# Query latent moved out of the first loop, the section behind it ordered by the scheduler, three gates early

## Chip, cores and metric

The kernel runs on one core of one Trainium2 chip. The metric is the device time of one execution in microseconds (us). All shapes are written partitions x elements; everything is stored as 32-bit floats.

## The reference

One layer of a diffusion block over 512 tokens of width 1024, with 256 context tokens. Cut to what matters here:

```
hx = rms_norm(x) * (1 + scale) + shift          # shift, scale = silu(c) @ w_mod, per channel
hc = rms_norm(ctx) * (1 + scale_c) + shift_c
conv_x, qa, kva, kr, gates = split(hx @ w_in)   # 2048, 384, 256, 64, 2048 columns
kva_c, kr_c = hc @ w_in[:, kv and kr columns]
q   = rms_norm(qa)  @ w_uq                      # 8 heads, 128 plain + 64 rotary
k,v = rms_norm(kva) @ w_ukv                     # 8 heads, keys and values, also for kva_c
att = softmax(q k) v @ w_o
u   = a * sigmoid(g);  y = silu(layer_norm(conv31(u))) @ w_pw
x  += m2 * ((sigmoid(g_conv) * y + sigmoid(g_mla) * att) @ w_out)
x  += m5 * swiglu(rms_norm(x) * (1 + m4) + m3);   out = rms_norm(x)
```

## The kernel before

Channels lie on partitions in tiles of 128, tokens along the free axis. Every product is made of three matmuls: weight and activation are each split into a high part (float32r, made by ScalarE, line 116 for weights) and a low part (the rest, made by VectorE, line 120), and `mm3` (L131) adds high*high, high*low and low*high. A weight of 128x1024 is loaded by SP into one of three raw buffers (`wr`), then split into two `wh` and two `wl` tiles of 512; with W_BUFS = 6 there are three such sets in all. The tag `x` of PSUM has 4 buffers of 512, the tag `s` 2 of 1024. A tile's buffer comes free when its last reader is done.

Order of work. Inside `manual_schedule` (L516 to L749) each engine runs the instructions in the order of the text. Outside it the order is made at build time by the framework's scheduler: the place in the text is the importance, and of the instructions whose operands and buffer are there by the scheduler's own estimate the most important is queued next on its engine. Each engine then runs its queue strictly in that order, SP's and POOL's DMA issues included.

The stages around the change:

- *Start* (L517 to L543). SP loads x, the row of c and, for k = 0 to 3, `load_mod(k)`: two halves of w_mod0, one tile of w_mod1 and one of w_q. ScalarE and VectorE square and add x; PE runs 34 warming matmuls (`warm`), sums the squares (`colsum`, L181), makes the shift of tile 0 and 1 with matmuls of 2 columns (`shift_dots`, L261, 16 instructions each) and spreads 1/rms over the partitions (`spread`, L171). Nine more warming matmuls stand ahead of the loop.
- *First loop* (L545 to L587), k = 0 to 7. VectorE and ScalarE make tile k of hx (L563, L564, L570); VectorE makes the scale of the next tile as a row dot product (L257); PE adds 18 matmuls (L572, L583, L585) to six accumulators `accx`: two for the query latent (one more at accx[5]), two for the kv latent, one for the rotary key. w_q therefore has 768 columns. One group of shift dots stands in each step.
- *Section behind it* (L588 to L749), written out by hand: squares, sums and 1/rms of the kv and query latents (`squares`, `added`, `diag`, `bcast` at L625, `latent_t` at L634, `latent_lo` at L641), the rotary key (L404, L419), the two convolution inputs u0 and u1 (`conv_steps`, L301; 48 matmuls each at L298) pumped in pieces between them, eight row dots for the context scale (`ctx_dots`, L593), the context tiles `hcs` (L712, L715, L718), two gates (`gate_steps`, L488) whose result goes to DRAM through POOL (L493), the context latent `pkv` and key `pkr`, and the first head's query, keys and values (`prep_qr`, `prep_qn`, `prep_kx`, `prep_kc`, `prep_v`).
- *Heads* (L752 to L771): scores, taps of the convolution, attention. Behind them (L773 to L803) five gates of the attention, the mean over the convolution (L790), the other six gates of the convolution and the norm; `spill` is read back at L787.

Of the kernel before, what the change touches and what calls it, by code (L numbers as in the profile page):

```python
# [10 lines left out]
F32 = mybir.dt.float32  # L11
F32R = mybir.dt.float32r
# [6 lines left out]
P = 128  # L19
# [14 lines left out]
WK_AT = (2, 5)  # L34
# [6 lines left out]
EARLY = 2  # L41
# [12 lines left out]
def block_kernel(ctx: ExitStack, tc: tile.TileContext, I, out):  # L54
# [461 lines left out]
    with tc.manual_schedule(engines={ET.PE, ET.DVE, ET.Activation, ET.Pool, ET.SP}):  # L516
# [18 lines left out]
        r = rstd_cols(st, D, 4)  # L535
        scale_dot(0)
        shift_dots(0)
        w = w_slots(768)
        w_hi(w, wq[0])
        ss = shift_scale(0)  # L540
        bc = spread(r, 4, tiny)
        shift_dots(1)
        warm(WARM[1])  # L543
        rx = slot()
        for k in range(KD):  # L545
# [7 lines left out]
            if k == 4:  # L553
# [6 lines left out]
                load_c += [load_w(I["w_in"][3 + KD + 1])]  # L560
# [7 lines left out]
            if nxt:  # L568
                scale_dot(k + 1)
            dve.scalar_tensor_tensor(out=hl, in0=t, scalar=ss[:, 0:1], in1=hh.bitcast(F32), op0=ALU.add, op1=ALU.subtract)  # L570
            for j in range(6):
                pe.matmul(accx[j], lhsT=wc(w[0], j * P), rhs=hh, start=k == 0, stop=False)  # L572
            if nxt:
                w2 = w_slots(768)
# [7 lines left out]
            for j in range(6):  # L582
                pe.matmul(accx[j], lhsT=wc(w[1], j * P), rhs=hh, start=False, stop=False)  # L583
            for j in range(6):
# [3 lines left out]
        mds = [load_md(k) for k in range(4)]  # L588
        load_c.append(load_w(I["w_in"][3 + 1]))
        act.activation(ccrow, ccrow, AF.Silu)  # L590

        def ctx_dots():
            for k in range(KD):  # L593
                row_dot(mds[k], ccrow, mod_s[:, 24 + k:25 + k])
                if k + 4 < KD:
                    mds.append(load_md(k + 4))
                yield

        dots = ctx_dots()


        def squares(srcs, n):
            o = []
            for p_ in srcs:
                sq = slot(n=n)
                act.activation(sq, p_, AF.Square)
                o.append(sq)
            return o

        def added(o):  # L610
            for sq in o[1:]:
                dve.tensor_tensor(out=o[0], in0=o[0], in1=sq, op=ALU.add)
            return o[0]

        def diag(r, n):
            dg = slot(n=n)
            dve.tensor_tensor(
                out=dg.rearrange("p (b j) -> p b j", b=n // P),
                in0=ident.unsqueeze(1).to_broadcast([P, n // P, P]),
                in1=r.unsqueeze(2).to_broadcast([P, n // P, P]), op=ALU.mult)  # L620
            return dg

        def bcast(dg, n):
            bc = tiny(n)
            pe.matmul(bc, lhsT=ones, rhs=dg, start=True, stop=True)  # L625
            o = slot(n=n)
            act.copy(o, bc)  # L627
            return o

        def latent_t(srcs, g, bc, dst, n):  # L630
            ts = []
            for i, s_ in enumerate(srcs):
                t = slot(n=n)
                dve.scalar_tensor_tensor(out=t, in0=s_, scalar=v(g, i), in1=bc, op0=ALU.mult, op1=ALU.mult)  # L634
                act.copy(dst[i][0], t)
                ts.append(t)
            return ts

        def latent_lo(ts, dst):
            for i, t in enumerate(ts):  # L640
                dve.tensor_tensor(out=dst[i][1], in0=t, in1=dst[i][0].bitcast(F32), op=ALU.subtract)  # L641

        for n_, lst in ((2, kva), (3, qa)):
            for _ in range(n_):
                lst.append((slot(F32R), slot(F32R)))
        krh, krl = slot(F32R), slot(F32R)
        krc = slot(F32R)
        for _ in range(2):
            h_ = slot(F32R)
            kvac.append((h_[:, 0:C], h_[:, C:2 * C]))  # L650

        misc = tiny()
        st_kv, st_q, st_c, st_c2 = misc[:, 0:4], misc[:, 4:8], misc[:, 8:10], misc[:, 10:12]
        raw8 = []
        steps = conv_steps(0, cw[0], cw[1])
        u0 = next(steps)
        kq = squares(accx[2:4], S)
        qq = squares([accx[5], accx[0], accx[1]], S)
        q2 = slot()
        act.copy(q2, accx[5])  # L660
        kq = added(kq)
        qq = added(qq)
        pump(steps, 12)
        colsum(st_kv, kq, 4, True, True)
        r_kv = rstd_cols(st_kv, 256, 4)
        tk = rope_ts(accx[4])
        pump(steps, 6)
        colsum(st_q, qq, 4, True, True)
# [516 lines left out]
```

## Time and profile before

| what | value |
|---|---|
| median of 3 runs | 1047.76 us (1047.34 to 1049.23) |
| profiled execution: its own time | 1044.45 us |
| profiled execution: span of the core | 1042.7 us |
| mean granted TensorE clock | 0.985 of full |

The span is what the trace covers; the execution's own time is 1.75 us more. A line of a timeline gives start, duration, engine, line of the code, operation, out<-in, shape and count; in square brackets stands how long the engine had stood idle and who ended that. A line of a table by windows gives for each engine the busy time and (x) the number of instructions, then the granted TensorE clock as a share of full speed, the busy share of the DMA engines and their GB/s.

### The profile page before, as it was taken

The page shows a single profiled execution, that of the slowest core. Times are in us where ns is not written, and L with a number is a line of the kernel's source. Part 1 is how long each engine was busy: PE and PEld are TensorE (multiplying, and loading weights), DVE is VectorE, ACT ScalarE, POOL GpSimd, SP SyncE. Part 2 cuts the span into 40 slices and gives each one's busy share as a digit, 9 for nine tenths or more (in the row PEclk, how much of TensorE's full clock was granted, in tenths as well). Part 3 has the DMA queues.
Part 4 walks back from the last instruction along what each step waited for, and adds up shares of the span by engine and source line. Part 5 has one row for each costly group of instructions (what it writes and reads, how often), then busy time and mean ns, then how long its engine had stood idle before and what let it go on. Part 6 is the DMA issues. An engine that isn't in the chain of part 4 may idle for free.

```text
span 1042.7 us, 14009 instructions
## 1 busy us (share of the span) xinstructions
PE 1008.4 (97%) x5178; PEld 854.9 (82%) x5178; DVE 554.7 (53%) x994; ACT 438.3 (42%) x818; POOL 150.6 (14%) x294
## 2 busy tenths in 40 slices
PE   8997999999999999997999999999999999999996
PEld 7885788888888887886878888988888888888886
DVE  5655774555555455426887775744643333433332
ACT  4244365555555556533382233443333333322322
POOL 0000301443443525530000000300000000000000
PEclk8998999999999999999999999999999999999998
DMA  9931742644644616753637654133632222333312
GB/s 343 369 110 40 241 128 76 151 128 121 161 114 128 163 41 160 187 135 112 202 119 254 221 165 150 62 102 104 219 101 92 90 102 95 87 91 108 91 56 81
DMA packets 52852, 143.40 MB, mean 138 GB/s; under 512 B 8880, under 2 KB 11056, under 8 KB 52784
## 3 DMA queue, kind: packets, MB, share of 16 engines
q1 hardware_dynamic: 42384, 116.54, 34.5%
q0 software_dynamic: 10400, 25.97, 10.4%
q8 instruction: 41, 0.67, 0.3%
q14 instruction: 27, 0.22, 0.1%
HBM read 114.42 MB, written 2.62 MB: 112 GB/s over the span
## 4 chain that ended last, share of the span: by engine, by line
PE 88%; DVE 3%; DMA 3%; issue 2%; ACT 2%; POOL 1%; SPq 0%; POOLq 0%; DVEq 0%; ACTq 0%
PE px L132 13%; PE px L133 12%; PE px L134 12%; PE ps L133 9%; PE ps L132 9%; PE ps L134 9%; PE px L298 8%; PE ps L455 3%; PE px L475 2%; PE ps L456 1%; PE px L264 1%; DMA ur<-u 1%; DMA a<-e 1%; PE px L419 1%; PE px L183 1%
## 5 line engine op out<-in xcount | busy, mean ns | idle before, releaser
L120 DVE TENSOR_TENSOR wl<-wr,wh 128x512 fp32r<-128x512 f32 (+2 forms) x284 | 189.9, 676 | 255.4 <-ACT wh L116 248.4
L116 ACT CAST wh<-wr 128x512 fp32r<-128x512 f32 (+2 forms) x290 | 174.4, 610 | 312.2 <-PE ps L133 144.5
L132 PE MATMUL px<-a,wh 128*128 128x512 f32 (+1 forms) x591 | 218.6, 371 | 0.6 <-ACT a L99 0.6
L133 PE MATMUL px<-a,wh 128*128 128x512 f32 (+1 forms) x591 | 217.0, 368 | 2.1 <-DVE a L718 2.1
L134 PE MATMUL px<-a,wl 128*128 128x512 f32 (+1 forms) x591 | 216.8, 367 | 0.0
L133 PE MATMUL ps<-a,wh 128*128 128x512 f32 (+1 forms) x376 | 141.6, 377 | 0.8 <-DVE a L925 0.8
L132 PE MATMUL ps<-a,wh 128*128 128x512 f32 (+1 forms) x376 | 141.5, 376 | 0.0
L134 PE MATMUL ps<-a,wl 128*128 128x512 f32 (+1 forms) x376 | 141.2, 375 | 0.0
L133 PEld LDWEIGHTS px<-a,wh 128*128 128x128 f32 x591 | 111.5, 189 | 22.3 <-DVE a L718 2.7
L132 PEld LDWEIGHTS px<-a,wh 128*128 128x128 f32 x591 | 111.6, 189 | 20.5 <-ACT a L99 1.4
L134 PEld LDWEIGHTS px<-a,wl 128*128 128x128 f32 x591 | 111.5, 189 | 18.2
L168 POOL TENSOR_TENSOR s<-s,mhalf 128x2 f32<-128x2 f32 (+1 forms) x10 | 9.0, 904 | 646.7 <-DVE s L166 646.7
L298 PE MATMUL px<-a,wh 128*128 128x512 f32 x288 | 91.9, 401 | 0.4 <-ACT a L627 0.4
L318 POOL DMA_DIRECT2D ur<-u x128 | 67.9, 537 | 121.2 <-issue 59.5
L133 PEld LDWEIGHTS ps<-a,wh 128*128 128x128 f32 x376 | 70.7, 188 | 14.3 <-DVE a L925 1.5
L134 PEld LDWEIGHTS ps<-a,wl 128*128 128x128 f32 x376 | 70.8, 188 | 12.8
L132 PEld LDWEIGHTS ps<-a,wh 128*128 128x128 f32 x376 | 70.8, 188 | 12.7
L332 POOL DMA_DIRECT2D a<-e x128 | 63.0, 498 | 90.8 <-ACT e L330 69.8
L298 PEld LDWEIGHTS px<-a,wh 128*128 128x128 f32 x288 | 54.6, 193 | 12.6 <-ACT a L627 1.1
L455 PE MATMUL ps<-a,a 128*128 128x512 f32 x160 | 58.2, 400 | 0.0
L298 PE MATMUL px<-a,wl 128*128 128x512 f32 x144 | 57.7, 401 | 0.0
L206 DVE SCALAR_TENSOR_TENSOR a<-p,sc,a 128x512 f32<-128x512 f32 x56 | 40.7, 748 | 19.3 <-DMA p<-in_w_mod_dram 19.1
(199 smaller groups left out, 1436.6 us busy)
## 6 DMA issues: line engine op xcount, KB each, us to landing
wr<-in_w_dram SPq DMA_DIRECT2D x60, 512.0 KB, 3.5
wr<-in_w_in_dram SPq DMA_DIRECT2D x35, 512.0 KB, 4.7
ur<-u POOLq DMA_DIRECT2D x128, 130.0 KB, 3.6
p<-in_w_mod_dram SPq DMA_DIRECT2D x64, 256.0 KB, 4.2
md<-in_w_mod_dram SPq DMA_DIRECT2D x16, 512.0 KB, 6.3
a<-e POOLq DMA_DIRECT2D x128, 64.0 KB, 2.0
a<-in_w_mod_dram SPq DMA_DIRECT2D x16, 256.0 KB, 7.2
wr<-in_w_dwx_dram SPq DMA_DIRECT2D x8, 512.0 KB, 4.0
```

The source lines that it names most:

```text
L116: act.copy(h, raw[:, i * WB:i * WB + h.shape[-1]])
L120: (eng or dve).tensor_tensor(out=l, in0=raw[:, i * WB:i * WB + h.shape[-1]], in1=h.bitcast(F32), op=ALU.subtract)
L132: pe.matmul(ps, lhsT=wh, rhs=ah, start=first, stop=False)
L133: pe.matmul(ps, lhsT=wh, rhs=al, start=False, stop=False)
L134: pe.matmul(ps, lhsT=wl, rhs=ah, start=False, stop=last)
L183: pe.matmul(ps[:, b:b + 1], lhsT=sq[:, b * P:(b + 1) * P], rhs=ones[:, 0:1], start=first and b == 0, stop=last and b == nb - 1)
L206: dve.scalar_tensor_tensor(out=acc[e], in0=md, scalar=sc[:, 2 * kc:2 * kc + 1], in1=acc[e], op0=ALU.mult, op1=ALU.add)
L298: pe.matmul(ps, lhsT=l, rhs=r, start=k == 0 and i == 0, stop=k == n - 1 and i == 2)
L318: pool.dma_start(out=ur[32 * s_:32 * s_ + 32].bitcast(F32), in_=u[32 * g:32 * g + 32, :, 8 * s_:8 * s_ + UW].bitcast(F32))
L332: pool.dma_start(out=parts[j][32 * g:32 * g + 32, :], in_=e[32 * j:32 * j + 32, j:j + S])
L455: pe.matmul(s[:, 0:512], lhsT=l[:, q0:q0 + P], rhs=rx_, start=i == 0, stop=i == 4)
L475: pe.transpose(pt[:, qb * P:(qb + 1) * P], ps_[qb][:, kb * P:(kb + 1) * P], ident)
```

## The change

In the first loop the accumulators of the query latent are gone: `accx` has three entries (two kv, one rotary key), the weight is `w_kv` with 384 columns, and a step has 9 matmuls. The shift dots of tile k + 1 stand in step k ahead of its matmuls (before: those of tile k + 2, in the middle of step k); tile 1's stood ahead of the loop before. Nine warming matmuls move ahead of `spread`, three more stand ahead of the loop. The query latent is made behind the loop by three ordinary products (`gemm`) with tiles `w_qa` of 128x1024, whose raw loads are issued in step 4; each result is squared and copied from PSUM. Loads of the convolution's weights in the loop are gone.

`manual_schedule` now ends with the loop. The section behind it stands in the order: kv latent and rotary key, query latent, context (row dots, `hcs`, pkv, pkr), both convolution inputs whole, `prep(0)`, and `EARLY` = 3 gates whole; the third gate (24 matmuls) leaves the stage behind the heads. No piece is pumped between others by hand.

```diff
-EARLY = 2
+EARLY = 3
...
-        t = wide()
-        sp.dma_start(out=t, in_=I["w_q"][k])
+        t = wide()[:, 0:384]
+        sp.dma_start(out=t, in_=I["w_kv"][k])
...
-    ab = (ps_s(), ps_s())
-    accx = [ab[j // 2][:, (j % 2) * 512:(j % 2) * 512 + 512] for j in range(4)] + [ps_x(), ps_x()]
+    ab = ps_s()
+    accx = [ab[:, 0:512], ab[:, 512:1024], ps_x()]
...
+        shift_dots(0)
+        warm(WARM[1])
+        w = w_slots(384)
+        w_hi(w, wq[0])
+        bc = spread(r, 4, tiny)
         scale_dot(0)
-        shift_dots(0)
-        w = w_slots(768)
-        w_hi(w, wq[0])
         ss = shift_scale(0)
-        bc = spread(r, 4, tiny)
-        shift_dots(1)
-        warm(WARM[1])
+        warm(WARM[2])
...
-            if k == 3:
+            if k == 4:
+                raw_q = [load_w(I["w_qa"][j]) for j in range(3)]
+                sp.dma_start(out=cst[:, 128:1152], in_=I["cst"][:, 128:1152])
                 ccrow = row_tile(1)
-                sp.dma_start(out=cst[:, 128:1152], in_=I["cst"][:, 128:1152])
-                load_c = [load_w(I["w_in"][3 + o]) for o in (KD, 0)]
...
             if nxt:
+                shift_dots(k + 1)
                 scale_dot(k + 1)
...
-            for j in range(6):
+            for j in range(3):
                 pe.matmul(accx[j], lhsT=wc(w[0], j * P), rhs=hh, start=k == 0, stop=False)
...
-            if k + 2 < KD:
-                shift_dots(k + 2)
-            if k >= KD - 2:
-                cw.append(split_w(load_c[k - KD + 2]))
...
+    colsum(st_kv, added(squares(accx[0:2], S)), 4, True, True)
+    wqa = [split_w(raw_q[0])]
+    dg_kv = diag(rstd_cols(st_kv, 256, 4), S)
+    tk = rope_split(rope_ts(accx[2]))
...
+    bc_kv = bcast(dg_kv, S)
+    latent_lo(latent_t(accx[0:2], "g_kv", bc_kv, kva, S), kva)
+    qsrc, qq = [], []
+    for j in range(3):
+        ps = ps_x()
+        gemm(ps, wqa[j], hx)
+        if j < 2:
+            wqa.append(split_w(raw_q[j + 1]))
+        qq += squares([ps], S)
+        t = slot()
+        act.copy(t, ps)
+        qsrc.append(t)
+    colsum(st_q, added(qq), 4, True, True)
+    mds = [load_md(k) for k in range(4)]
+    cq = squares(ctxs, C)
+    for i, sq in enumerate(cq):
+        colsum(st_c, sq, 2, i == 0, i == KD - 1)
+    bc_q = bcast(diag(rstd_cols(st_q, 384, 4), S), S)
+    latent_lo(latent_t(qsrc, "g_q", bc_q, qa, S), qa)
+    rc = bcast(diag(rstd_cols(st_c, D, 2), C), C)
+    for k in range(KD):
+        row_dot(mds[k], ccrow, mod_s[:, 24 + k:25 + k])
+        if k + 4 < KD:
+            mds.append(load_md(k + 4))
...
+    for k in range(KD):
...
+        act.activation(hcs[k][0], t, AF.Identity, bias=ssc[:, k:k + 1])
...
+    pkv = ps_x()
+    for j in range(2):
+        gemm(pkv[:, j * C:(j + 1) * C], wtile(I["w_in"][1 + j]), hcs)
...
+    pkr = ps_x(C)
+    gemm(pkr, wtile(I["w_in"][0]), hcs)
+    split(pkr, krc[:, 0:C], krc[:, C:2 * C])
+    us = []
+    for i in range(2):
+        it = conv_steps(i)
+        us.append(next(it))
+        pump(it, 99)
+    prep(0)
+    for i in range(EARLY):
+        gate_ws[i] = wtile(I["w_in"][19 + i])
+        pump(gate_steps(i), 99)
...
-        for i in range(2, 7):
+        for i in range(EARLY, 7):
             sg_conv.append(gate(19 + i, o_t[6]))
```

## Rows read from the trace of the kernel before

**Rows 1.** The page: its head and the chain that ended last, by engine.
```profile
span 1042.7 us, 14009 instructions
...
PE 88%; DVE 3%; DMA 3%; issue 2%; ACT 2%; POOL 1%; SPq 0%; POOLq 0%; DVEq 0%; ACTq 0%
```

**Rows 2.** Busy time by window: first loop, section behind it, densest 20 us of VectorE.
```profile
26.00:69.60 43.60, 43.60 (x241) 37.65 (x241) 25.26 (x47) 14.83 (x37) 0.00 (x0) 1.00 0.77 282
69.60:148.24 78.64, 68.68 (x357) 57.41 (x355) 56.34 (x104) 37.82 (x77) 14.49 (x28) 0.93 0.43 128
...
100.00:120.00 20.00, 19.51 (x78) 15.98 (x79) 17.18 (x34) 5.19 (x10) 5.61 (x12) 0.89 0.83 251
```

**Rows 3.** The chain in order of time, one step of the loop: start, us, what.
```profile
51.35 1.68 PE px L264 x16
...
57.27 1.68 PE px L264 x16
```

**Rows 4.** Timeline of PE behind the section's first part: matmul spacing, idle time, small sums.
```profile
83.42 3.63 PE L183 MATMUL px<-ones,a 128*128 128x1 f32 x32
...
93.39 0.39 PE L298 MATMUL px<-a,wl 128*128 128x512 f32 x1
...
94.07 0.39 PE L298 MATMUL px<-a,wl 128*128 128x512 f32 x1
100.49 1.22 PE L625 MATMUL px<-a,ones 128*128 128x256 f32 x2 [6.03 <-DVE a L617]
...
123.76 0.28 PE L132 MATMUL px<-a,wh 128*128 128x256 f32 x1
125.94 0.38 PE L133 MATMUL px<-a,wh 128*128 128x256 f32 x1 [1.90 <-DVE a L718]
```

**Rows 5.** Busy time by window: granted clock (third column from the end) at three places.
```profile
16.00:17.00 1.00, 0.00 (x0) 0.00 (x0) 0.96 (x4) 0.87 (x3) 0.00 (x0) 0.50 1.03 414
...
25.00:26.00 1.00, 1.00 (x7) 1.00 (x7) 1.00 (x3) 0.00 (x0) 0.00 (x0) 0.51 1.05 396
...
88.00:89.00 1.00, 1.00 (x4) 0.81 (x3) 0.00 (x0) 0.00 (x0) 0.00 (x0) 0.50 0.83 225
...
103.00:104.00 1.00, 1.00 (x3) 0.78 (x3) 1.00 (x3) 0.00 (x0) 0.00 (x0) 0.50 0.89 311
```

**Rows 6.** Timeline of PE ahead of the loop.
```profile
13.39 1.93 PE L264 MATMUL px<-sc,a 128*128 128x2 f32 x16
17.05 2.07 PE L178 MATMUL px<-t,ones 128*128 128x512 f32 x2 [1.74 <-DVE t L173]
18.92 3.41 PE L264 MATMUL px<-sc,a 128*128 128x2 f32 x16
22.19 4.06 PE L274 MATMUL px<-ones 128*128 128x128 f32 x18
26.00 1.17 PE L572 MATMUL ps<-a,wh 128*128 128x512 f32 x4
```

**Rows 7.** Groups of VectorE in 69.60:148.24: line, operation, count | busy us, mean ns.
```profile
L120 DVE TENSOR_TENSOR wl<-wr,wh 128x512 fp32r<-128x512 f32 x22 | 14.3, 687 | 4.7 <-ACT wh L116 4.6
L257 DVE SCALAR_TENSOR_TENSOR md<-md,row 128x1024 f32<-128x1024 f32 x8 | 9.6, 1222 | 0.1
L712 DVE SCALAR_TENSOR_TENSOR t<-a,ssc,a 128x256 f32<-128x256 f32 x8 | 3.8, 478 | 0.0
```

**Rows 8.** Timeline of POOL: the root of two sums.
```profile
95.95 0.70 POOL L168 TENSOR_TENSOR s<-s,mhalf 128x2 f32<-128x2 f32 x1 [18.36 <-DVE s L166]
...
132.86 1.10 POOL L168 TENSOR_TENSOR s<-s,mhalf 128x2 f32<-128x2 f32 x1 [3.62 <-DVE s L166]
```

**Rows 9.** Timelines behind the heads: PE at the mean, VectorE's last sum, PE's next sum.
```profile
487.12 2.05 PE L790 MATMUL px<-a,ones 128*128 128x512 f32 x2 [5.54 <-DVE a L782]
...
498.40 0.69 DVE L797 TENSOR_TENSOR a<-a,t 128x512 f32<-128x512 f32 x1
...
516.79 0.95 PE L183 MATMUL px<-ones,a 128*128 128x1 f32 x8
```

More of the change, by code (lines that the diff above doesn't have):

```diff
@@ L610, in added @@
[L610 to L656, printed above, removed]
@@ L686, in block_kernel @@
-        pump(steps, 99)
-        raw8 += [load_w(I["w_in"][19 + i]) for i in range(EARLY)]
-        tq = latent_t([accx[0], accx[1], q2], "g_q", bc_q, qa, S)
-        r_c = rstd_cols(st_c, D, 2)
-        cw += [split_w(load_c[3])]
-        latent_lo(tq, qa)
-        dg_c = diag(r_c, C)
-        pump(dots, 4)
-        gate_ws[0] = split_w(raw8[0])
-        load_w8 = [load_w(I["w_in"][1]), load_w(I["w_in"][2]), load_w(I["w_uq"][0, :, 0:D]), load_w(I["w_in"][0]),
-                   load_w(I["w_uv"][0], 512)]
@@ L725, in block_kernel @@
-        pump(gates, 99)
-        pkv = ps_x()
-        for j in range(2):
-            gemm(pkv[:, j * C:(j + 1) * C], wk[j], hcs)
-        wu = split_w(load_w8[2])
-        kq = squares([pkv[:, 0:C], pkv[:, C:2 * C]], C)
-        pump(steps, 5)
-        colsum(st_c2, added(kq), 2, True, True)
-        r_c2 = rstd_cols(st_c2, 256, 2)
-        wkr = split_w(load_w8[3])
-        dg_c = diag(r_c2, C)
-        pump(steps, 99)
-        terms = prep_qr(*wu)
-        prep_qn(*wu, 0)
-        bc_c = bcast(dg_c, C)
@@ L740, in block_kernel, with squares @@
-        pkr = ps_x(C)
-        gemm(pkr, wkr, hcs)
-        latent_lo(latent_t([pkv[:, 0:C], pkv[:, C:2 * C]], "g_kv", bc_c, kvac, C), kvac)
-        wv = split_w(load_w8[4], 512)
-        split(pkr, krc[:, 0:C], krc[:, C:2 * C])
-        stack_q(0, terms)
-        kx = prep_kx(*wu, 768)
-        stack_q(1, terms)
-        prep_kc(*wu, 768, 0, kx)
-        prep_v(*wv, 0)
-    us = [u0, u1]
+    def squares(srcs, n):
+        o = []
+        for p_ in srcs:
+            sq = slot(n=n)
+            act.activation(sq, p_, AF.Square)
+            o.append(sq)
+        return o
@@ new lines, in added, with diag, bcast @@
+    def added(o):
+        for sq in o[1:]:
+            dve.tensor_tensor(out=o[0], in0=o[0], in1=sq, op=ALU.add)
+        return o[0]
+    def diag(r, n):
+        dg = slot(n=n)
+        dve.tensor_tensor(
+            out=dg.rearrange("p (b j) -> p b j", b=n // P),
+            in0=ident.unsqueeze(1).to_broadcast([P, n // P, P]),
+            in1=r.unsqueeze(2).to_broadcast([P, n // P, P]), op=ALU.mult)
+        return dg
+    def bcast(dg, n):
+        bc = tiny(n)
+        pe.matmul(bc, lhsT=ones, rhs=dg, start=True, stop=True)
+        o = slot(n=n)
+        act.copy(o, bc)
+        return o
@@ new lines, in latent_t, with latent_lo @@
+    def latent_t(srcs, g, bc, dst, n):
+        ts = []
+        for i, s_ in enumerate(srcs):
+            t = slot(n=n)
+            dve.scalar_tensor_tensor(out=t, in0=s_, scalar=v(g, i), in1=bc, op0=ALU.mult, op1=ALU.mult)
+            act.copy(dst[i][0], t)
+            ts.append(t)
+        return ts
+    def latent_lo(ts, dst):
+        for i, t in enumerate(ts):
+            dve.tensor_tensor(out=dst[i][1], in0=t, in1=dst[i][0].bitcast(F32), op=ALU.subtract)
+    for n_, lst in ((2, kva), (3, qa)):
+        for _ in range(n_):
+            lst.append((slot(F32R), slot(F32R)))
@@ new lines, in block_kernel @@
+    krh, krl = slot(F32R), slot(F32R)
+    krc = slot(F32R)
+    for _ in range(2):
+        h_ = slot(F32R)
+        kvac.append((h_[:, 0:C], h_[:, C:2 * C]))
+    misc = tiny()
+    st_kv, st_q, st_c, st_c2 = misc[:, 0:4], misc[:, 4:8], misc[:, 8:10], misc[:, 10:12]
+    colsum(st_kv, added(squares(accx[0:2], S)), 4, True, True)
+    wqa = [split_w(raw_q[0])]
+    dg_kv = diag(rstd_cols(st_kv, 256, 4), S)
+    tk = rope_split(rope_ts(accx[2]))
+    act.copy(stackr, mats)
+    rope_sum(accx[2], tk, 0)
@@ new lines, in block_kernel @@
+    act.copy(krh, accx[2])
+    dve.tensor_tensor(out=krl, in0=accx[2], in1=krh.bitcast(F32), op=ALU.subtract)
+    bc_kv = bcast(dg_kv, S)
+    latent_lo(latent_t(accx[0:2], "g_kv", bc_kv, kva, S), kva)
+    qsrc, qq = [], []
+    for j in range(3):
+        ps = ps_x()
[7 more added lines that the diff above has]
+    colsum(st_q, added(qq), 4, True, True)
@@ new lines, in block_kernel @@
+    mds = [load_md(k) for k in range(4)]
[9 more added lines that the diff above has]
+            mds.append(load_md(k + 4))
+    ssc = cp.tile([P, 16], F32, name="ssc")
```

99 lines of the change are left out of this document (17 added, 82 removed).

## The prediction

> **What bounds the kernel now.** I read the page first: of the chain that ended last 88% is PE, so time is won or lost where PE stands or runs slowly [rows 1]. Then the busy time by window: the first loop has PE busy 43.6 of 43.6 us at full clock; the section behind it, up to the first scores at 148.24 us, has PE busy 68.7 of 78.6 us at a mean clock of 0.93, with VectorE (DVE) busy 56.3 us, 72% [rows 2]. Then the timeline of PE for the section: one stand of 6.03 us behind 94.07 us and one of 1.90 us, both ended by DVE [rows 4], and stretches at half clock, the lower of its two levels (1.2 of 2.4 GHz), behind 32 sums of one column (3.63 us) and behind the long stand [rows 4, 5]. Last the stage behind the heads, where a gate is taken out [rows 9].
>
> Prices on PE: three matmuls of 512 columns take 94.07 - 93.39 = 0.68 us, one 0.227 [rows 4]; one of 256 about half, 0.12; a sum instruction 3.63 / 32 = 0.113 [rows 4]. A loop step lasts 57.27 - 51.35 = 5.92 us, 1.68 of it shift dots [rows 3].
>
> **The change part by part.** *Start of the loop.* PE's clock was already at half in 16 to 17 us, when PE stood 1.74 us for the spread, and was full again at 26 us, behind the nine warming matmuls (18 instructions, 4.06 us) [rows 5, 6]. The change puts these nine into that stand, at 15.3 us. Taken at half clock they end at 19.4; I take the clock as full from there, as it was behind them before. Then the spread (1.0, half its row), three warming matmuls (0.7) and tile 1's dots (1.7) give the first matmul at 22.7 us, not 26.0. Bounds: no gain, if the clock stays low, and 5.1 us, if it never falls.
>
> *The loop.* A step loses 9 x 0.227 us on PE and keeps its dots: 9 x 0.227 + 0.1 + 1.68 = 3.8 us (0.1 is half of what the old step has beyond its parts). Six steps with dots and two of 2.05 without give 26.9; the last tile's hx is 0.9 us late, since only nine matmuls cover its chain. The loop ends at 22.7 + 26.9 + 0.9 = 50.5 us. Before, it ended at 69.6, which without the 72 query matmuls (16.3 us) is 53.3: **-2.8 us**. What hides the rest: DVE was busy 25.3 us in 43.6, and 3.3 us a step fit under 3.8 once a weight split is half as wide; if the query weights' splits are pushed in between (four at 0.65 us), up to 2.6 us come on top. The loads, 1.25 MB a step, need 3.1 us at the 396 GB/s of the old start [rows 5].
>
> *Work behind the loop.* PE had 63.0 us there: 144 matmuls of L298 (32.7), 24 others of 512 (5.4), 114 of 256 (13.7), 52 sums (5.9), broadcasts and rotary sums (5.3). So 78.6 - 63.0 = 15.6 us were lost: 6.0 and 1.9 in stands, some 3.7 in about 7.4 us at half clock [rows 4, 5], and 4.0 in small ones. Now 16.3 us of query matmuls and one gate of 24 (5.45) come in. The query matmuls are already counted above. The gate goes out behind the heads, where PE stands for nothing else after the mean, and where the chain that the gates cover was done at 499 us, while PE asked for it at 516.8 [rows 9]: five gates cover it as six did. In and out cancel: zero. Without that cover the 5.45 us would be lost. The third gate's store and reload are two DMAs of 256 KB that nothing waits for: zero, as the two before. On SP's queue the convolution's loads leave the loop and three query loads enter; 1.5 MB behind the last w_mod tile, not ahead of it.
>
> *The new wait.* This is the large term. The text deals the three weight sets out in its own order: w_qa three times, then kv and key of the context, then the convolutions. A set that a query tile frees goes to a context weight, which keeps it until `hcs` is there. From the end of the query products until the first context product is done no convolution and no gate has a set, so PE's filler is behind a lock. On PE's queue the context products stand first, and the convolutions, the first head's query, keys and values and so the scores wait behind them. What DVE must finish before the last `hcs`: 30 operations of 512 columns (kv and key 11, query 9, six query splits, four context splits) at 0.65 us (14.3 / 22) make 19.5; eight row dots 9.6; `hcs` twice 3.8, since the low parts cost as the first; small ones 1.7 [rows 7]. That is 38.4, less 1.3 for one query weight split in the loop: 37.1 us. DVE was busy 72% over this section and 86% in its densest 20 us [rows 2]; I take the middle, 79%, since the row dots can fill gaps: the last `hcs` at 47.0 us behind the loop. PE has until then, and 1.1 us after: 72 query matmuls 16.3, 48 sums 5.4, broadcasts and rotary sums 3.0, context products 72 x 0.12 = 8.6, in all 33.4. PE loses 47.0 + 1.1 - 33.4 = **14.7 us**. The bounds: 3.5 us (DVE always busy and two splits in the loop, 35.8 us) and 20.8 us (72%, nothing in the loop: 53.1).
>
> *Beside it.* The first convolution weight can be split only when the first context product is done: 2.4 us for split and handover, of which 0.7 lie under the second product: 1.7. The stand brings the half clock back: some 3.8 us, 1.9 lost, as at 100 to 105 us; the 32 sums cost the same 1.8 as before [rows 4, 5]. Of the 4.0 us of small stands I keep 2.8, since the context's last chain lies beside convolutions now. Loss behind the loop: 14.7 + 1.7 + 1.9 + 1.8 + 2.8 = 22.9 us, against 15.6: **+7.3 us**.
>
> *The roots on POOL.* Each of four sums ends in a root on POOL: 0.70 us with DVE idle, 1.10 us while DVE splits a weight [rows 8]. A denser DVE may cost 0.4 us for each of the two ahead of `hcs`; inside the bounds, so zero. The Trainium skill ("SBUF — State Buffer", section "Summary: rules for kernel authors") has a DVE instruction with two SBUF inputs and a POOL instruction that reads SBUF exclude each other for the whole instruction. This speaks against a denser DVE; a root that waits for a whole row dot would be 1.2 us later, the two of them 2.4, and the sum +6.9 in place of +4.5. The row shows a third of that, and the row decides.
>
> **Sum.** -2.8 + 7.3 = **+4.5 us**: the profiled execution would go from 1044.45 to 1048.95 us. It lies 3.3 us below the median of the runs, 1047.76; on the median the forecast is **1052.3 us**.
>
> **Rivals.** *DVE is dense (faster).* [...] Loss 3.5 + 1.7 + 1.8 + 2.8 = 9.8, sum -2.8 - 5.8 = -8.6: 1039.2 us. It decides from 87% of busy DVE on, where the sum is zero: the wait is then 10.2 us. For it: 86% was reached [rows 2], and the 6.03 us stand of the hand order goes. Against: DVE waits in strict order for ScalarE's high parts, 4.7 us in 22 splits [rows 7].
>
> *The two cancel (same).* DVE between 83 and 92%: within 2.1 us of 1047.76.
>
> *A queue stands at its head (slower still).* The scheduler's order is made from estimates. Behind the heads, where it already has its way, PE stood 5.54 us at the mean with gates left to do, and came back at half clock [rows 9]. The same once at a sum or a row dot ahead of its load costs 5.5 + 1.9 = 7.4 more: 1059.7 us.
>
> *The lock doesn't close.* If convolution weights get sets ahead of the context's, PE has its filler and the loss is 1.8 + 2.8: 1047.76 - 2.8 - 11.0 = 1034 us. Against: the text's order is the importance, and the loads wait for nothing but a buffer.
>
> **The numbers.** Forecast 0.40, standing queue 0.14, dense DVE 0.28, open lock 0.05, cancelling 0.13. So slower 0.54, faster 0.33, same 0.13; same means within 0.2%, 2.1 us, about what a measurement of this kernel can tell from no change. The range reaches from the dense case, 1039, to a little past the standing queue, 1062, which leaves out the open lock and the worst ends. The likeliest case's own range is 1050 to 1057 us, from DVE at 82% to 72%.
>
> **What would show it.** Right: the first loop matmul near 22.7 us, a loop step of 3.8 us, the loop's end near 50 us; one stand of PE of over 10 us between the last query matmul and the last context matmul, ended by DVE's low parts of `hcs`, with no L298 matmul ahead of it and a half clock behind it; the stage behind the heads 5.5 us shorter. Wrong: L298 matmuls between the query products and the context, a step well over 3.8 us, PE standing for a load in the loop, or the clock at half throughout the loop, since its share of 512-column matmuls falls.

## The result and the profile after

| | before | after |
|---|---|---|
| median | 1048.49 us (4 runs, 1047.34 to 1051.8) | 1074.05 us (4 runs, 1073.26 to 1074.47) |
| ratio, 95% interval | | 1.0238 [1.0213, 1.0262] |
| profiled execution, span | 1044.45, 1042.7 us | 1073.26, 1071.2 us |
| mean granted clock | 0.985 | 0.966 |
| first loop, first to last matmul | 26.00 to 69.60 us | 23.77 to 66.30 us |
| first scores | 148.24 us | 181.70 us |

Slower, as forecast, but by 25.6 us where 4.5 were forecast, and outside the range. The page of after, its head and its chain:

```profile
span 1071.2 us, 14038 instructions
...
PE 82%; DMA 7%; DVE 4%; issue 2%; POOL 2%; ACT 2%; SPq 0%; POOLq 0%; DVEq 0%; ACTq 0%
```

PE's share of the chain fell from 88% [rows 1] to 82%, and loads rose from 3% to 7%. Where the time went shows in the busy time by window (first loop, section behind it, and two stretches of 20 us inside them):

```profile
23.77:66.30 42.53, 33.52 (x170) 28.68 (x169) 25.04 (x48) 14.48 (x36) 0.18 (x2) 0.80 0.73 269
66.30:181.70 115.40, 99.16 (x451) 81.88 (x451) 61.90 (x113) 44.19 (x87) 13.94 (x26) 0.84 0.37 111
...
40.00:60.00 20.00, 13.03 (x48) 11.29 (x49) 7.27 (x14) 4.10 (x10) 0.18 (x2) 0.57 0.63 231
...
100.00:120.00 20.00, 12.28 (x40) 9.10 (x41) 12.63 (x26) 7.61 (x15) 0.87 (x2) 0.50 0.01 2
```

Beside [rows 2]: the loop has 170 matmul instructions instead of 241 and is hardly shorter. Without the 72 query matmuls the old loop would have ended at 53.3 us (the prediction's working); the new one ends at 66.30, **+13.0**. The section has the prediction's 63.0 + 16.3 + 5.45 = 84.8 us of work for PE in 115.4 us: a loss of 30.6 where before it was 15.6, **+15.0**. Together 28.0; the spans differ by 28.5. The section's loss has two parts. PE's idle time (length less busy time) rose from 78.64 - 68.68 = 10.0 to 115.40 - 99.16 = 16.2 us. The other part is half clock: in the 20 us from 100 us on alone, PE was busy 12.28 us at 0.50, which costs 6.1 us. An estimate for the whole section, from PE's busy time and granted clock in windows of half a microsecond, gives 13.2 us lost to half clock, against 3.7 before.

**The loop.** The timeline of PE, first matmuls of tiles 2 to 7:

```profile
31.52 0.70 PE L570 MATMUL ps<-a,wh 128*128 128x512 f32 x2
35.38 0.70 PE L570 MATMUL ps<-a,wh 128*128 128x512 f32 x2
46.97 1.22 PE L570 MATMUL ps<-a,wh 128*128 128x512 f32 x2 [7.58 <-ACT mod_s L265]
54.24 1.20 PE L570 MATMUL ps<-a,wh 128*128 128x512 f32 x2
60.23 0.71 PE L570 MATMUL ps<-a,wh 128*128 128x512 f32 x2
63.92 0.73 PE L570 MATMUL ps<-a,wh 128*128 128x512 f32 x2 [1.39 <-ACT a L561]
```

Ahead of tile 4 PE stands 7.58 us, and the steps behind it last 7.27 and 5.99 us, where a step ahead of it lasts 3.86. The bracket names ScalarE; what it was doing stands in its own timeline:

```profile
45.67 0.62 ACT L641 CAST stackr<-a 128x512 fp32r<-128x512 f32 x1 [9.35 <-DMA a<-in_cst_dram]
46.20 0.72 ACT L561 ACTIVATE a<-t,s 128x512 fp32r<-128x512 f32 x1
```

and the load that it waited for in the chain in order of time:

```profile
36.90 8.75 DMA a<-in_cst_dram
```

`act.copy(stackr, mats)` rounds the rotary matrices, which are first needed behind the loop. It now stands in the text behind the hand-ordered block (L641), so the scheduler places it, and it placed it in ScalarE's queue directly ahead of tile 4's hx (L561). Its load, issued at 36.90 us behind three query weights, the constants and the context's row (512 KB each), landed 8.75 us later. In-order ScalarE waited, and the whole loop with it.

**The section.** PE's timeline between the query products (dense from 73.7 to 91.1 us) and the first convolution matmul:

```profile
93.16 5.76 PE L182 MATMUL px<-ones,a 128*128 128x1 f32 x40 [1.86 <-DVE a L595]
100.99 2.07 PE L608 MATMUL px<-a,ones 128*128 128x512 f32 x2 [2.07 <-DVE a L600]
107.99 1.22 PE L608 MATMUL px<-a,ones 128*128 128x256 f32 x2 [4.93 <-DVE a L600]
110.73 0.58 PE L131 MATMUL px<-a,wh 128*128 128x256 f32 x1 [1.52 <-ACT a L678]
...
131.28 0.63 PE L297 MATMUL px<-a,wh 128*128 128x512 f32 x2
```

No convolution matmul (L297) comes ahead of the context, as forecast, but the stands are several, and VectorE isn't full: in the first 24.80 us, to 91.10, it was busy 21.00, but from 91.10 to 110.70 us only 7.48 of 19.60. Its timeline there:

```profile
100.24 0.69 DVE L600 TENSOR_TENSOR a<-cst,s 128x512 f32<-128x512 f32 x1 [1.06 <-POOL s L167]
103.72 2.08 DVE L617 SCALAR_TENSOR_TENSOR a<-a,vec,a 128x512 f32<-128x512 f32 x3 [2.78 <-ACT a L610]
105.71 1.89 DVE L624 TENSOR_TENSOR a<-a,a 128x512 fp32r<-128x512 f32 x3
107.52 0.42 DVE L600 TENSOR_TENSOR a<-cst,s 128x256 f32<-128x256 f32 x1
109.65 1.27 DVE L675 SCALAR_TENSOR_TENSOR t<-a,ssc,a 128x256 f32<-128x256 f32 x3 [1.72 <-ACT a L610]
```

The context's diagonal (L600, 128x256) is 0.42 us of work and ran at 107.52, because the query's latent (L617, L624) stands ahead of it in VectorE's queue, and that had to wait for its broadcast and ScalarE's copy of it. The context's sums themselves came only at 93.16, behind the query's. It is a serial chain in the order of the text, and PE is at half clock through most of it.

**Behind the heads** the stand at the mean is what it was [rows 9]:

```profile
519.76 2.05 PE L739 MATMUL px<-a,ones 128*128 128x512 f32 x2 [5.54 <-DVE a L731]
544.06 0.95 PE L182 MATMUL px<-ones,a 128*128 128x1 f32 x8
```

The mean comes 32.6 us later than before, the first scores 33.5, and from the mean to the next sum it is 24.30 us instead of 29.67: the gate taken out gives its 5.4 us back there.

### The profile page after: what moved, and what is told of

It is laid out like the page before. It is cut to its first block, busy times and chain, and to the rows that moved or that the text cites. A ratio compares the mean times of both kernels' runs of the same rounds, so it can differ in the third digit from the quotient of the medians.

```text
span 1071.2 us, 14038 instructions
## 1 busy us (share of the span) xinstructions
PE 1022.1 (95%) x5184; PEld 865.0 (81%) x5184; DVE 555.0 (52%) x992; ACT 441.1 (41%) x818; POOL 151.7 (14%) x295
## 4 chain that ended last, share of the span: by engine, by line
PE 82%; DMA 7%; DVE 4%; issue 2%; POOL 2%; ACT 2%; SPq 0%; POOLq 0%; DVEq 0%; ACTq 0%
PE px L131 12%; PE px L132 12%; PE px L133 11%; PE px L297 10%; PE ps L132 9%; PE ps L131 9%; PE ps L133 9%; PE ps L454 2%; DMA a<-in_w_mod_dram 2%; PE px L474 1%; PE ps L455 1%; DMA ur<-u 1%; DMA a<-e 1%; DMA p<-in_w_mod_dram 1%; PE px L182 1%
## 5 line engine op out<-in xcount | busy, mean ns | idle before, releaser
L119 DVE TENSOR_TENSOR wl<-wr,wh 128x512 fp32r<-128x512 f32 (+1 forms) x290 | 194.4, 676 | 277.6 <-ACT wh L115 270.9
L115 ACT CAST wh<-wr 128x512 fp32r<-128x512 f32 (+1 forms) x296 | 179.2, 611 | 353.1 <-PE px L132 149.5
L131 PE MATMUL px<-a,wh 128*128 128x512 f32 (+1 forms) x607 | 228.3, 377 | 2.1 <-ACT a L678 1.5
L132 PE MATMUL px<-a,wh 128*128 128x512 f32 (+1 forms) x607 | 226.6, 373 | 1.8 <-DVE a L99 1.5
L133 PE MATMUL px<-a,wl 128*128 128x512 f32 (+1 forms) x607 | 225.8, 372 | 0.0
L131 PEld LDWEIGHTS px<-a,wh 128*128 128x128 f32 x607 | 117.5, 194 | 24.1 <-ACT a L678 2.2
L132 PEld LDWEIGHTS px<-a,wh 128*128 128x128 f32 x607 | 117.4, 193 | 22.9 <-DVE a L99 2.1
L133 PEld LDWEIGHTS px<-a,wl 128*128 128x128 f32 x607 | 117.3, 193 | 18.9
L297 PE MATMUL px<-a,wh 128*128 128x512 f32 x304 | 93.9, 390 | 0.0
L297 PEld LDWEIGHTS px<-a,wh 128*128 128x128 f32 x304 | 56.1, 188 | 11.6
L297 PE MATMUL px<-a,wl 128*128 128x512 f32 x152 | 59.2, 389 | 0.0
L99 DVE TENSOR_TENSOR pl<-px,ph 128x512 fp32r<-128x512 f32 x48 | 32.7, 689 | 31.1 <-ACT ph L98 30.6
```

The lines of the kernel that those rows point to most:

```text
L99: dve.tensor_tensor(out=lo, in0=src, in1=hi.bitcast(F32), op=ALU.subtract)
L115: act.copy(h, raw[:, i * WB:i * WB + h.shape[-1]])
L119: (eng or dve).tensor_tensor(out=l, in0=raw[:, i * WB:i * WB + h.shape[-1]], in1=h.bitcast(F32), op=ALU.subtract)
L131: pe.matmul(ps, lhsT=wh, rhs=ah, start=first, stop=False)
L132: pe.matmul(ps, lhsT=wh, rhs=al, start=False, stop=False)
L133: pe.matmul(ps, lhsT=wl, rhs=ah, start=False, stop=last)
```

## The experiments

All twelve, with before timed beside each; e1 is the base of most. "Section" is from the last loop matmul to the first scores, in the profiled execution.

| run | median us | ratio to before, 95% | section us |
|---|---|---|---|
| after | 1074.05 | 1.0238 [1.0213, 1.0262] | 115.4 |
| e1 copy behind the loop | 1057.76 | 1.0084 [1.0053, 1.0115] | 114.6 |
| e2 two gates early | 1072.64 | 1.0231 [1.0196, 1.0267] | 109.0, a gate less |
| e3 = e1, conv weights first | 1061.04 | 1.0109 [1.0077, 1.0142] | 114.0 |
| e4 = e1, context rows first | 1059.64 | 1.0101 [1.0064, 1.0138] | 114.2 |
| e5 = e1, conv 0 first | 1057.91 | 1.0081 [1.0049, 1.0113] | 114.0 |
| e6 = e1, section rewritten | 1037.10 | 0.9887 [0.9864, 0.9909] | 92.3 |
| e7 load issued earlier | 1061.62 | 1.0139 [1.0088, 1.0190] | 113.8 |
| e8 = e1, first part of e6 | 1054.39 | 1.0052 [1.0035, 1.0068] | 108.4 |
| e9 = e6 without that part | 1040.29 | 0.9924 [0.9900, 0.9948] | 95.0 |
| e10 = e6, copy in the loop | 1047.70 | 1.0004 [0.9975, 1.0033] | 89.7 |
| e11 = e1, context's root first | 1055.72 | 1.0067 [1.0046, 1.0087] | 110.9 |
| e12 = e6, query's root earlier | 1032.86 | 0.9853 [0.9831, 0.9875] | 87.3 |

### e1: the copy back in the hand-ordered block

```diff
         act.activation(ccrow, ccrow, AF.Silu)
+        act.copy(stackr, mats)
...
     tk = rope_split(rope_ts(accx[2]))
-    act.copy(stackr, mats)
```

> The changed kernel with one line moved: the rounding of the rotary matrices (act.copy(stackr, mats)) written at the end of the hand-ordered block, behind the context row's Silu, so that ScalarE meets it when the loop is done. Theory A (a late load at the head of ScalarE's queue): the stand of 7.58 us ahead of tile 4's products goes, the clock stays full to the end of the loop, the steps stay at 3.9 us and the loop ends at 51 to 53 us instead of 66.3; the rest keeps its length, so 1074.05 - 13 to 14 = 1060 to 1061 us. Rival B (the stand is the throttle's doing, the copy only happens to be there): the loop still has steps of 6 to 7 us at half clock, at most 2 us gained, 1072 or more. Rival C (what the loop gives is lost again in front of the context's rows, whose loads come when they come): the loop ends at 52 but the first score comes less than 5 us earlier, 1069 or more.

16.3 us less on the medians. The windows (first loop, section) and PE's last step:

```profile
23.54:52.81 29.27, 27.91 (x170) 24.05 (x169) 25.05 (x48) 14.57 (x36) 0.18 (x2) 1.00 1.02 391
52.81:167.43 114.62, 97.64 (x451) 80.94 (x451) 62.00 (x113) 44.54 (x87) 13.57 (x26) 0.85 0.39 112
...
50.44 0.74 PE L570 MATMUL ps<-a,wh 128*128 128x512 f32 x2 [1.36 <-ACT a L561]
```

The loop is 29.27 us at full clock instead of 42.53 at 0.80, 13.3 us less, and the section keeps its length; the spans differ by 13.1, and the rest of the 16.3 lies between profiled executions and medians. This is Theory A, with a median 2 us under its 1060 to 1061. One line, whose own work is 0.62 us, carries 13 to 16 of the 25.6 us lost.

### e7: the load issued two steps earlier

```diff
+            if k == 2:
+                mats = slot()
+                sp.dma_start(out=mats, in_=I["cst"][:, 1152:1664])
             if k == 4:
...
-                mats = slot()
-                sp.dma_start(out=mats, in_=I["cst"][:, 1152:1664])
```

> The changed kernel with the load of the rotary matrices issued two steps of the loop earlier (with tile 2 instead of tile 4, ahead of tile 6's weights); the rounding copy stays in the scheduler's hands, and it now stands one tile earlier in ScalarE's queue, ahead of tile 3's rows instead of tile 4's. Theory A1 (the scheduler puts the copy where it takes the load to have landed, which is too early by the time that the load stands behind those in front of it): the stand only moves one tile ahead and is as long, 5 to 9 us, the clock falls behind it as before, 1070 to 1076 us. Theory A2 (the load was only late in this place): it has landed when ScalarE comes to the copy, no stand, loop end at 52 to 54 us, 1058 to 1062 us.

ScalarE's row of the copy, then PE's first matmuls of tiles 3 and 4:

```profile
35.20 0.62 ACT L642 CAST stackr<-a 128x512 fp32r<-128x512 f32 x1 [4.29 <-DMA a<-in_cst_dram]
```

```profile
36.50 0.97 PE L571 MATMUL ps<-a,wh 128*128 128x512 f32 x2 [2.52 <-ACT mod_s L265]
41.95 0.70 PE L571 MATMUL ps<-a,wh 128*128 128x512 f32 x2
```

The copy moved one tile ahead with its load, and still waits for it: the mechanism of A1. But PE's stand was 2.52 us, and behind it only one step was slow, 5.45 us at a mean clock of 0.69, so the time is that of A2. The 2.5 us of the stand and the 1.6 us of the slow step make up the 3.9 us by which e7's median lies over e1's. The load was issued 8.0 us earlier (28.93 us) and took 6.25 us instead of 8.75; bringing it forward shortened the stand, but didn't remove it. Why the load was quicker isn't shown by a run of its own; in the 3 us ahead of it 1.2 MB were issued, in after 2.5 MB. One of e7's four runs took 1069.99 us, at a mean clock of 0.966 where the others have 0.973 to 0.977.

### e2: the gate

```diff
-EARLY = 3
+EARLY = 2
```

> The changed kernel with two gates ahead of the heads instead of three, as the kernel before has it. If the third gate's move is worth nothing, as the prediction had it: the first score comes 5.4 to 6 us earlier than 181.7 us, the end of the heads keeps the place of that gate, and the total stays at 1074 +- 1 us. Rival: the third gate ahead of the heads costs a stand of its own (a spill, a weight set), then 1068 to 1070 us; or it fills a hole there, then 1077 to 1079.

1072.64 (1073 to 1075 expected), ratio 1.0231 against 1.0238. The two intervals reach some 3 us to either side, so the gate's move is worth nothing that can be measured. The profiled executions agree: the first score comes 9.85 us earlier than in after, 3.5 of them from the loop, which has one slow step instead of two, and 6.4 from the section. From the mean to the next sum it is 30.16 us instead of 24.30, so 5.9 come back, and the stand at the mean is 5.54 us with six gates as with five.

### e3, e4, e5: single pieces of the section moved

e3 deals out the two weights of the first convolution ahead of the context's:

```diff
+    cw0 = [wtile(I["w_in"][3 + KD]), wtile(I["w_in"][3])]
     colsum(st_q, added(qq), 4, True, True)
...
-        it = conv_steps(i)
+        it = conv_steps(i, *(cw0 if i == 0 else ()))
```

> The kernel of e1 with the two weight tiles of the first convolution dealt directly behind the query products in the text, ahead of the context's weights; the products themselves stay where they are in the text. Theory A (weight sets dealt in the text's order keep other products out of the gap of 91 to 131 us, where TensorE has some 15 us of work in 40): the first convolution's 10.9 us of products run in that gap, 8 to 11 us less than e1, 1049 to 1053 us. Theory B (the gap is a serial chain behind the query's: the context's sums, root, broadcast and row tiles stand in the text behind the query's, and the scheduler's order leaves nothing else in front of the context's products): the convolution's products still stand behind the context's products on TensorE, e1 +- 1.5 us.

e4 writes the context's sums, root, row dots and rows ahead of the query products:

```diff
-    qsrc, qq = [], []
-    for j in range(3):
...
     mds = [load_md(k) for k in range(4)]
     cq = squares(ctxs, C)
...
+    qsrc, qq = [], []
+    for j in range(3):
...
     pkv = ps_x()
```

> The kernel of e1 with the context's sums, root, broadcast, row dots and rows written ahead of the query's latent in the text; the context's products stay behind it. Theory B (serial chain in order of the text): the query's 17 us of products cover the context's chain, the rows are there when the query's products end, the gap of 40 us shrinks by 10 to 15 us: e1 - 8 to - 13, 1048 to 1052 us. Theory A (weight sets): the gap only changes its place, since no set for other products comes free until the context's products are done: e1 +- 3. Rival: the row dots on VectorE, now ahead of the query's weight splits, hold back the query's products, and the section becomes longer: e1 + 3 or more.

e5 writes the whole first convolution ahead of the query's and the context's roots:

```diff
+    us = []
+    it = conv_steps(0)
+    us.append(next(it))
+    pump(it, 99)
     bc_q = bcast(diag(rstd_cols(st_q, 384, 4), S), S)
...
```

> The kernel of e1 with the whole first convolution (weights, 48 products, its row tile) written directly behind the query products, so that it stands ahead of the query's and the context's broadcasts and the context's products in the order of importance. Theory B (the section's loss is a serial chain with nothing written ahead of it that could fill it; the order of the text decides): its 10.9 us of products fill the stands of 77.6 to 98 us, whose idle time and half clock hold some 14 us; the first score comes 8 to 12 us earlier than in e1, 1046 to 1050 us. Theory A' (the chain's length isn't TensorE's to cover, because VectorE and ScalarE then have the convolution's splits ahead of the context's rows): the context's rows move back by as much, 1055 to 1060 us. Less than 3 us of difference to e1 would mean that the stands only change place.

None of the three gains; the section stays at 114 us in each. e3: the splits of these weights were done by 77.3 us, and the first convolution matmul came at 115.06, behind the context's. So the weight sets, the prediction's lock, are not what keeps PE from its filler. e4: the context's chain then runs ahead of the query products, with stands of 4.83 and 2.40 us in front of them; the chain was moved, not covered. e5 shows why filling alone doesn't help. Two windows, the first from where the convolution and the context's sums alternate on PE, and VectorE's timeline in the second:

```profile
77.00:91.00 14.00, 14.00 (x50) 12.15 (x51) 2.21 (x5) 2.48 (x6) 2.11 (x2) 0.53 0.06 22
...
96.00:105.00 9.00, 2.04 (x4) 0.52 (x3) 7.11 (x13) 4.22 (x9) 6.16 (x12) 0.82 0.66 161
```

```profile
98.01 2.07 DVE L618 SCALAR_TENSOR_TENSOR a<-a,vec,a 128x512 f32<-128x512 f32 x3
100.00 1.89 DVE L625 TENSOR_TENSOR a<-a,a 128x512 fp32r<-128x512 f32 x3
101.80 0.42 DVE L601 TENSOR_TENSOR a<-cst,s 128x256 f32<-128x256 f32 x1
```

The scheduler interleaved the convolution with the context's sums. PE had run at full clock from 57.6 us (1.00 to 77.0); in this mixture it fell to 0.53 while PE was busy 14.00 of 14.00 us, and it was full again only at 91.5, 5 us behind the last of these sums. Then the broadcasts came behind the convolution on PE's queue, the context's diagonal behind the query's latent on VectorE's, and PE stood 5.52 us once more. The filler was spent ahead of the chain instead of beside it: in the section PE is idle 13.9 us instead of e1's 17.0, but loses 14.0 us to half clock instead of 11.4 (both clock figures estimated as above).

### e11: two statements exchanged

```diff
+    rc = bcast(diag(rstd_cols(st_c, D, 2), C), C)
     bc_q = bcast(diag(rstd_cols(st_q, 384, 4), S), S)
     latent_lo(latent_t(qsrc, "g_q", bc_q, qa, S), qa)
-    rc = bcast(diag(rstd_cols(st_c, D, 2), C), C)
```

> The kernel of e1 with two statements exchanged: the context's root, diagonal and broadcast written ahead of the query's root, broadcast and latent. In e1 TensorE has the context's broadcast at 95.42 us, 4.93 us after the query's, because VectorE's queue holds the query's latent (which waits for its broadcast's copy) ahead of the context's diagonal. Serial chain by the order of the text: the context's broadcast comes directly behind the sums, at 88 to 89 us, its products start 5 to 7 us earlier, and the query's latent is made beside them, 1051 to 1053 us. Rival (the row tiles wait for something else, their row dots or loads): e1 +- 1.5 us.

2.0 us less on the medians, where 5 to 7 were expected. Both broadcasts stand at 87.49 us now, 7.9 us earlier for the context's, and the stand of 4.93 us is gone. But the first context product came at 94.66 us behind a stand of 3.85 (e1: 98.16): the query's casts (1.94 us) now lie in ScalarE's queue ahead of the context's high parts, and its latent (3.97 us) in VectorE's ahead of the low parts. The term was right, but most of it moved on to the next place in the queues.

### e6, e8, e9, e12: the section written in another order

e6 has the same instructions and weights as e1. Its text, cut to the order:

```diff
+    wqa = [split_w(r) for r in raw_q]
+    sq = added(squares(accx[0:2], S))
+    query(0)
+    colsum(st_kv, sq, 4, True, True)
+    dg_kv = diag(rstd_cols(st_kv, 256, 4), S)
+    tk = rope_split(rope_ts(accx[2]))
+    cq = squares(ctxs, C)
+    query(1)
+    rope_sum(accx[2], tk, 0)
...
+    dg_c = diag(rstd_cols(st_c, D, 2), C)
+    query(2)
...
+    rc = bcast(dg_c, C)
...
+    pump(it0, 24)
...
+    colsum(st_q, sqq, 4, True, True)
+    dg_q = diag(rstd_cols(st_q, 384, 4), S)
+    pump(it0, 99)
+    bc_q = bcast(dg_q, S)
```

`query(j)` is the change's loop body, `it0` the first convolution; behind this come pkv, pkr, the context latent's sums, the second convolution's first product, the broadcast, its second product. e8 is e1 with the part down to `rope_sum`, `bc_kv` and `query(2)` alone; e9 is e6 with the key latent's chain back in front.

> The kernel of e1 with the section behind the loop written in another order, nothing else: the three query products first and the key latent's sums, turned copy and broadcast between them; the context's sums and row dots between the second and the third; the first convolution's two products around the query's sums; then the context's products, its rotary product, and the second convolution's first product ahead of the context latent's broadcast. Theory B (order of the text): TensorE is dense from the end of the loop (52.8 us) on; 84.8 us of work and 5 to 9 us of stands give the first score at 143 to 147 us against 167.4 in e1, so 1033 to 1038 us, under the kernel before. Rival (VectorE and ScalarE bound the section, 37 us of VectorE's work on the way to the context's rows): some 10 us of it come back as waits for the context's rows, 1043 to 1049. Rival (weights: six half sets and SyncE's loads set the pace): the convolution's products wait on splits, 1048 or more.

> The kernel of e1 with the first part of e6's order alone: the query products written ahead of and between the key latent's sums, turned copy and broadcast; all behind the query's last product is e1's. If the section's loss adds up by places: the 8.4 us between the loop's end and the first query product (52.8 to 61.2 us in e1, some 3 to 4 us of it work) become dense, the query's products end 4 to 5 us earlier, and nothing behind them changes, 1052 to 1054 us. Rival (the chain behind the query's products, not TensorE, is what sets the first score, and it starts from something else than their end): e1 +- 1.5 us.

> The kernel of e6 with the key latent's sums, turned copy, broadcast and latent back ahead of the query products, as e1 has them; the context's sums between the query products, and the first convolution around the roots, stay. Adding up by places: 4 to 5 us more than e6, 1041 to 1043 us; with e8 it makes up the difference of e1 and e6 (20.7 us). If the two parts only work together, over 1047.

e6 is 20.7 us faster than e1 and beats the kernel before, by 1.1%; time and first score (145.48 us) lie where Theory B had them. The window of its section, and the two stands that are left:

```profile
53.17:145.48 92.31, 87.59 (x448) 73.77 (x446) 61.16 (x113) 43.46 (x87) 15.24 (x26) 0.96 0.48 139
```

```profile
91.11 1.10 PE L609 MATMUL px<-a,ones 128*128 128x512 f32 x2 [2.23 <-DVE a L601]
...
105.39 0.61 PE L182 MATMUL px<-ones,a 128*128 128x1 f32 x4 [2.49 <-DVE a L596]
```

The loss is 92.3 - 84.8 = 7.5 us instead of 29.8, and the clock 0.96 instead of 0.85: PE's idle time fell from 17.0 to 4.7 us, and the loss to half clock from 11.4 to 3.4 (estimated as above). VectorE has as much work as in e1 (61.2 against 62.0 us) and is no bound; from the loop's end to the last `hcs` (90.36 us) it is busy 30.53 of 37.19 us. On the medians the places add up: e8 takes 3.4 us off e1, e9 has 3.2 more than e6 and is 17.5 under e1; 3.4 + 17.5 = 20.9. Each of these differences is uncertain by some 3 us, and the sections of the table add up less well (6.2 + 19.6 = 25.8 for 22.3). So the first place was a little overpriced (4 to 5), and the large one is the context's chain with the convolution beside it. Either of these moved alone, in e4 and e5, gained nothing.

e12 takes up the two stands:

```diff
-    pump(it0, 24)
+    pump(it0, 12)
+    colsum(st_q, sqq, 4, True, True)
+    dg_q = diag(rstd_cols(st_q, 384, 4), S)
+    pump(it0, 12)
...
+    pump(it, 8)
     colsum(st_c2, sq2, 2, True, True)
     dg_c2 = diag(rstd_cols(st_c2, 256, 2), C)
-    pump(it, 24)
+    pump(it, 16)
```

> The kernel of e6 with its two remaining stands taken up: the query's sums and root in the middle of the first convolution's first product instead of between the two, and eight of the second convolution's products ahead of the context latent's sums. If both stands (2.23 and 2.49 us) are covered: 3 to 5 us less than e6, 1032 to 1034 us. Rival (VectorE's queue then stands at the query's diagonal with the context's rows behind it): e6 +- 1.5 us or more.

```profile
53.09:140.43 87.34, 86.09 (x446) 72.52 (x446) 60.84 (x113) 43.41 (x87) 15.63 (x26) 0.98 0.50 147
```

1032.86 us, 4.2 less than e6 and 1.5% under the kernel before: the fastest version found. The section loses 2.5 us.

### e10: both at once

e6 with the copy left to the scheduler, so that it stands ahead of tile 4 again:

```diff
-        act.copy(stackr, mats)
...
     tk = rope_split(rope_ts(accx[2]))
+    act.copy(stackr, mats)
```

> The section in e6's order, but the rounding of the rotary matrices left to the scheduler as in the changed kernel; it stands at the same place of ScalarE's queue, ahead of tile 4's rows. If loop and section are separate causes: 13 to 16 us more than e6, 1050 to 1053 us, with the same stand of some 7.5 us and half clock behind it. If the section's dense order takes up a part of what the loop loses (work that waited for nothing but the loop's time): 1043 to 1049.

10.6 us more than e6 (10.0 without the slowest run). PE's first matmuls of tiles 4 to 6, then two windows from that point to the loop's end, of e10 and of after:

```profile
45.92 1.22 PE L570 MATMUL ps<-a,wh 128*128 128x512 f32 x2 [8.10 <-ACT mod_s L265]
51.27 0.70 PE L570 MATMUL ps<-a,wh 128*128 128x512 f32 x2
55.14 0.70 PE L570 MATMUL ps<-a,wh 128*128 128x512 f32 x2
```

```profile
45.92:61.17 15.25, 14.95 (x73) 12.28 (x74) 12.03 (x22) 7.92 (x18) 0.18 (x2) 0.89 0.50 170
```

```profile
46.97:66.30 19.33, 17.90 (x68) 14.72 (x68) 12.08 (x22) 7.95 (x18) 0.18 (x2) 0.69 0.37 128
```

The stand is the same (8.10 and 7.58 us), the clock behind it isn't: here one step is slow (5.35 us), in after two (7.27 and 5.99). e10's ten runs reach from 1042.44 to 1060.53 us, while e6's four lie within 2.7, and the three above 1050 us have the lowest mean clocks (0.971 to 0.976, the others 0.982 or more). So the stand is the sure part of the loss, and half clock comes on top in varying size: the slow steps cost 1.5 us here (5.35 - 3.87) and 5.5 in after. The median, 1047.70, lies in the range of the second expectation, but its reason, a section that takes up a part of the loop's loss, isn't shown. The clock alone explains 4 us of the distance to the first. The section of e10 is 2.6 us shorter than e6's (89.7 against 92.3), in one profiled execution of each.

## Why the prediction was wrong in size

- **Start and step: near.** First matmul 23.77 us (22.7 forecast): the nine warming matmuls began at 15.77 instead of 15.3, and the clock, taken as full from 19.4, was 0.52 until the spread was done at 21.39. A step is 3.87 (3.8), and the loop of e1, with the same instructions, has a clock of 1.00, so the loop at half clock throughout, one of the signs of being wrong, did not come. In e1 the loop ends at 52.81, 2.3 us past the forecast: 0.8 from its start at 23.54, 0.4 from six steps of 3.87, 1.1 from the last two tiles (6.06 us for 5.0, 1.36 of it the wait that was set at 0.9).
- **"The loop ends at 50.5 us" failed by 15.8 us, and this is the larger miss.** The step counted the loads that enter the loop and DVE's splits, but took the loop's queues as written by hand. The change ends the hand order earlier, and with that a statement written behind the loop could be put into it. The prediction named the mechanism ("a queue stands at its head") and a sign of it ("PE standing for a load in the loop"), but put it behind the loop, gave it 7.4 us and a chance of 0.14. e1 measures it: 13.3 us in the profiled loops, of which 7.6 are the stand and 5.5 the two slow steps behind it (7.27 + 5.99 - 2 x 3.87).
- **The half clock behind the loop, left at what it was before, is the term that failed in "+7.3 us".** +15.0 came (+14.2 in e1). The sum set 1.9 + 1.8 = 3.7 us for it, and the estimate from the trace is 13.2 (11.4 in e1); the section's mean clock fell from 0.93 to 0.84. PE's idle time rose by 6.2 us (10.0 to 16.2), where the sum's stands rise by 7.3 (15.6 - 3.7 = 11.9 to 14.7 + 1.7 + 2.8 = 19.2).
- **The new wait: PE's idle time came near in size, but by luck, since the reason was wrong.** The first context product started 44.4 us after the loop's end and the last `hcs` was done at 50.4 (47.0 forecast), but not for 37.1 us of VectorE's work: it was busy 34.5 us of the 50.4, its row dots were done at 87.1 us, and it stood more than half of the 20 us ahead of the first `hcs`. The lock of weight sets fell with e3, VectorE's occupancy as the bound with e6. Shown instead, by e5, e11, e6 and e12: the text's order, which makes every engine's in-order queue, puts three sum-root-broadcast chains one behind the other with no product between their links.
- **The gate: right**, zero (e2); the chain at the mean was covered by five gates as by six.
- **The roots on POOL.** Zero was right for the sum. In after two roots took 1.67 us together with VectorE idle. e6 has the case that was argued over: its context root began at 68.78 us, 0.16 us into a row dot, and took 1.62 us, against 0.70 alone [rows 8], ending 0.55 us behind the row dot (the two lines under this paragraph). That is close to the rule in the Trainium skill ("SBUF — State Buffer", "Summary: rules for kernel authors"), a wait for the whole instruction, and further than the 0.4 us that I took from a weight split. That row fits the rule as well, and "a third" was a misreading: the split beside the root of 132.86 us [rows 8] began at 132.69 and lasts 0.65 us, so 0.48 of it were left. PE was on a broadcast and the third query product meanwhile, so it cost nothing.

```profile
68.62 1.23 DVE L256 SCALAR_TENSOR_TENSOR md<-md,row 128x1024 f32<-128x1024 f32 x1
```

```profile
68.78 1.62 POOL L167 TENSOR_TENSOR s<-s,mhalf 128x2 f32<-128x2 f32 x1 [8.62 <-DVE s L165]
```

- **Rivals.** Dense VectorE, and with it a faster kernel, was not to be had in this order (68% to the last `hcs`; 82% in e6). Its sum sets nothing for half clock, and no run shows that a wait of 3.5 us leaves the clock full: behind e7's stand of 2.52 us it was at half. "The lock doesn't close" gave 1034 us for a PE that always has filler; e6 and e12 reach 1037 and 1033 by exactly that, though not through the weight sets.

## What to carry to other kernels

When a hand-ordered stretch is cut short, go through every statement that falls out of it, the tiny ones too, and ask which load it waits for and in which queue it may be put ahead: 0.62 us of ScalarE's work cost 13 to 16 us here. Where the place in the text is the importance, write filler between the links of a chain (sum, root, broadcast, rows), in the order that each engine's queue shall have; filler ahead of the chain or weights alone gained nothing. Check the claim "the engine is full" in the stretch just ahead of the wait, not over the whole stage. And give half clock a price of its own for each stand and each run of small sums: in this section it cost nearly as much as PE's idle time.

## Not expected of the hardware

- A load of 128x512 (256 KB) took 8.75 us from issue to landing in after, while the DMA engines moved 384 GB/s, and 6.25 us in e7, where it was issued 8 us earlier.
- In e5 the clock fell from full to half with no stand ahead of it, where products of 512 columns alternate with one-column sums (0.53 from 77 to 91 us, PE busy 14.00 of 14.00; the last of the sums ended at 86.3).
- After nearly the same stand (7.58, 7.01 and 8.10 us in after, e2 and e10) the slow steps that followed differed: 7.27 and 5.99, 6.07, and 5.35 us. Behind e7's shorter stand, 2.52 us, the one slow step was 5.45 us. What decides it stays open.
